# RWKV head pairs: the bonus product placed behind the products of A, and GpSimd's zeros of the first head pair placed behind the spread of the norms

## The chip, the cores and the metric

The kernel runs on one core of a Trainium2 chip. The metric is the device time of one execution in microseconds (us), as the median over several runs. A profiled execution, taken separately, gives the trace.

The engines of the core are named as in the profile: PE is TensorE (PEld its weight loads), DVE is VectorE, ACT is ScalarE, POOL is GpSimd and SP is SyncE, which issues most DMAs.

## What is computed

One layer of a hybrid decoder: RWKV-7 time mixing and differential attention side by side, merged by gates, followed by an MLP. The change lies in the RWKV branch, in the norm of `kk` and in the bonus:

```
r, k, v, wd, ad, gd = jnp.split(Pr, RWKV_SPLITS, axis=-1)
...
kk = hs((k * lp['k_k']).astype(f32))
kk = kk / jnp.maximum(jnp.linalg.norm(kk, axis=-1, keepdims=True), 1e-12)
k = k.astype(f32) * (1.0 + (a - 1.0) * lp['k_a'].astype(f32))
S, y = rwkv7_scan(S0, hs(r), hs(decay), hs(k), hs(v), -kk, kk * hs(a))
...
bonus = jnp.sum(hs(r).astype(f32) * hs(k) * lp['r_k'].astype(f32), axis=-1, keepdims=True) * hs(v).astype(f32)
o = (y + bonus).reshape(B, T, W_A).astype(Pr.dtype) * g
```

`rwkv7_scan` is a recurrence over time with a 64 x 64 state per head. The bonus is needed only at the very end, where it is added to the normalised `y`.

## The kernel before

There are 512 prompt tokens and 64 sample tokens, 576 in a row (`NT`), with features on the partitions. The RWKV branch has eight heads of 64 features, handled as four head pairs `hp` of 128 partitions. The recurrence is done in nine chunks of 64 tokens. For each head pair the generator `rwkv(hp)`, in this order:

- squares `k` (`sq`), sums it over each head on TensorE (`pn`), brings the sums to the power -1/2 on GpSimd (`nr`, L760), spreads them over 64 features on GpSimd (`nb`, L763) and transposes them back on TensorE (`pk`, `pks`); VectorE multiplies them into `kk`, which shares the buffer of `sq`;
- makes the decay (`pw`, `u`, `cum`, `pe`, `pinv`) and the gate `a` (`pa`, `aa`), and the gated key `k2`;
- makes the bonus: `rkp` = r times r_k times k2 on VectorE, its sum over each head by a matmul with a block of ones (`pbn`, two halves), and `bv` = `pbn` times v on VectorE;
- makes the stacked factors `KB` and `ST` (two tiles `ST`, one for each parity of the head in the pair), whose unused rows GpSimd sets to zero (L818);
- makes the products A (`pA`, six banks of PSUM) on TensorE, and from each bank two masked pieces on VectorE: `ABR` and the other rows of `ST`;
- transposes v (`pV`, copied by ACT into `SVU`) and `KB` (`pK`, copied into `KBt`), multiplies the sample states (`pI`), and inverts small triangular blocks in a series of steps (`pW`, `pZ`, `pWc`, `pC`), into `TT`. Parts of `SVU` and `TT` are zeroed, or filled with an identity, by GpSimd (L871, L872, L923, L924).

When two head pairs are ready, `chain(pr)` walks the nine chunks (`pch`, `pY`). After that `pF` updates the sample states: `vm` on GpSimd, `pF` on TensorE, then the update on VectorE, a DMA out (`Ss`) and the DMA in of the next head pair's states.

Between these pieces TensorE works off a stream of dense projections of the gates (`ps_z`, `ps_g`, with weights split into `hi` and `lo`, and results evicted by VectorE into `Z` and `gg`). `take(n)` and `fill(n)` put n steps of the stream at a place of the program; `fill` also keeps them behind the last matmul. The order of instructions on each engine is set by a list scheduler, from the order of the code, from dependencies, and from `tc.issue_after(x)`, which keeps what is issued in its block behind `x` in the order. It adds no wait on the chip. So a piece of code that is moved can shift the order of all engines around it.

`bank` hands out PSUM banks from a ring of three; the stream's banks are a ring of two. `tmp` hands out buffers from a ring of six; `nb` and `vm` share a ring of three (tag G).

Of the kernel before, what the change touches and what calls it, by code (L numbers as in the profile page):

```python
# [8 lines left out]
F32 = mybir.dt.float32  # L9
# [6 lines left out]
P = 128  # L16
# [5 lines left out]
NT = NPR + NS  # L22
# [6 lines left out]
HALF = ((0, 288), (288, 288))  # L29
# [3 lines left out]
V_MU, V_W0, V_A0, V_KK, V_KA, V_RK, V_LW, V_LB, V_GM, V_GF, V_GO, V_SUB, V_END = (  # L33
    0, 14, 18, 22, 26, 30, 34, 38, 42, 50, 58, 66, 67)


C_ID, C_OB, C_M, C_MS, C_LM, C_I32, C_HS, C_SEL, C_MB, C_CM, C_END = (
    0, 128, 256, 384, 512, 672, 704, 706, 738, 746, 748)
# [3 lines left out]
def tile_hybrid_step(ctx, tc, xT, xsT, ktab, vtab, s0T, ptab, w_in, vecs, w2a2, g2, lamv,  # L42
# [3 lines left out]
    PE, VE, AE, GE = nc.tensor, nc.vector, nc.scalar, nc.gpsimd  # L46
    PS = bass.MemoryType.PSUM

    def pool(name, bufs=1, stack=ctx, **kw):
        return stack.enter_context(tc.tile_pool(name=name, bufs=bufs, **kw))  # L50
# [4 lines left out]
    ring = {"job": 0}  # L55

    def act(out, in_, func=AF.Copy, **kw):
        ring["act"] = AE.activation(out=out, in_=in_, func=func, **kw)  # L58

    def tt(out, a, b, op, eng=None):  # L60
        ins = (eng or VE).tensor_tensor(out=out, in0=a, in1=b, op=op)  # L61
        if eng is None:
            ring["tt"] = ins

    def stt(out, a, s, b, op0, op1):
        VE.scalar_tensor_tensor(out=out, in0=a, scalar=s, in1=b, op0=op0, op1=op1)
# [4 lines left out]
    def mm(out, lhsT, rhs, start=True, stop=True):  # L71
        ring["mm"] = PE.matmul(out=out, lhsT=lhsT, rhs=rhs, start=start, stop=stop)  # L72
        return ring["mm"]
# [17 lines left out]
    MUL, ADD, SUB, MAX = ALU.mult, ALU.add, ALU.subtract, ALU.max  # L91
# [9 lines left out]
    def bank(name):  # L101
        return psw.tile([P, 512], F32, tag="w", name=name)
# [9 lines left out]
    c = const.tile([P, C_END], F32, name="cst_sb")  # L112
    nc.scalar.dma_start(out=c, in_=cst)
    ident = c[:, C_ID:C_ID + P]
    onesblk = c[:, C_OB:C_OB + P]
# [18 lines left out]
    def v(i, n=1):  # L134
        return vec[:, i:i + n]
# [135 lines left out]
    with tc.tile_pool(name="xin", bufs=2, reuse_waits="tile") as xin:  # L271
# [6 lines left out]
        for k in range(0, KT, 4):  # L278
            for j in range(3):
                with prio(FEED + 1000 + 10 * k + j):  # L280
                    name = f"raw_{'qkv'[j]}0_{k}"
                    if k == 0:
                        raw = ring["pool"].tile([P, 4, P], F32, tag="raw", name=name, bufs=3)
                    else:
                        raw = zw.tile([P, 1 + NX], F32, tag="z" if j else "tz", name=name,
                                      bufs=2 if j else 1)[:, :4 * P].rearrange("p (k w) -> p k w", k=4)
# [378 lines left out]
    for h in range(HB):  # L665
        if h:
            qkv(h)
        for cc in range(2):
            GE.tensor_copy(
                out=qbd[64 * cc:64 * cc + 64, :, h, 8 * cc:8 * cc + 8],  # L670
                in_=qT[64 * cc:64 * cc + 64, h, NPR:].rearrange("p (b q) -> p b q", b=NB))
# [44 lines left out]
    rb_ = pool("rb_", 2, stack=rk, reuse_waits="tile")  # L716
    rt = pool("rt", 2, stack=rk, reuse_waits="tile")

    def ch(a):
        return a.rearrange("p (c t) -> p c t", t=64)  # L720

    def m3(ap_, n):
        q, w = ap_.shape
        return ap_.rearrange("p (o w) -> p o w", o=1).broadcast_to([q, n, w])
# [17 lines left out]
    def rwkv(hp):  # L742
# [3 lines left out]
        r, k, vv = Pt[hp], Pt[4 + hp], Pt[8 + hp]  # L746

        def tmp(tag, bufs=1):
            return rt.tile([P, NT], F32, tag="T", name=f"{tag}_{hp}", bufs=6)


        sq = tmp("sq")
        act(sq, k, AF.Square, scale=v(V_KK + hp))
        pn = bank(f"pn{hp}")
        for t, o in enumerate(toks):
            mm(pn[:, 2 * t:2 * t + 2], sq[:, o:o + P], c[:, C_HS:C_HS + 2])
        (fill if hp != 2 else take)(8)
        nr = stat.tile([P, 10], F32, tag="nr", name=f"nr{hp}")
# [1 line left out]
        GE.tensor_tensor(out=nr, in0=nr, in1=mhalf[:, :10], op=ALU.pow)  # L760

        nb = rt.tile([P, 5, P], F32, tag="G", name=f"nb{hp}", bufs=3)
        GE.tensor_copy(out=nb.rearrange("p t (a d) -> p (t a) d", a=2),  # L763
                       in_=nr.rearrange("p (a o) -> p a o", o=1).broadcast_to([P, 10, 64]))
        u = tmp("u")
        aa = tmp("aa")
        for t0, n in HALF:
# [31 lines left out]
        k2 = tmp("k2")  # L799
        act(k2, aa, AF.Identity, scale=ka2[:, hp:hp + 1], bias=ka2[:, 4 + hp:5 + hp])  # L800
        tt(k2, k2, k, MUL)
        rkp = tmp("rkp")
        stt(rkp, r, v(V_RK + hp), k2, MUL, MUL)
        bv = rb_.tile([P, NT], F32, tag="bv", name=f"bv{hp}", bufs=4)
        for t0, n in HALF:
            pbn = bank(f"pbn{hp}{t0}")
            mm(pbn[:, :n], onesblk, rkp[:, t0:t0 + n])
            tt(bv[:, t0:t0 + n], pbn[:, :n], vv[:, t0:t0 + n], MUL)


        KB = rt.tile([P, NCH, 2, 64], F32, tag="KB", name=f"KB{hp}", bufs=1)
        stt(aa, aa, 1.0, kk, ADD, MUL)
# [1 line left out]
        for par, rows in halves:  # L814
            stt(KB[rows, :, par], ch(aa)[rows], 0.5, ch(pinv)[rows], MUL, MUL)
            tt(KB[rows, :, 1 - par], ch(k2)[rows], ch(pinv)[rows], MUL)
            st = rb_.tile([P, NCH, 2, 64], F32, tag=f"ST{par}", name=f"ST{par}_{hp}")
            GE.memset(st[64 - 64 * par:128 - 64 * par], 0.0)  # L818
            stt(st[rows, :, 0], ch(kk)[rows], -1.0, ch(pm)[rows], MUL, MUL)
            tt(st[rows, :, 1], ch(r)[rows], ch(pe)[rows], MUL)  # L820
            ST.append(st)
# [4 lines left out]
        for par in range(2):  # L826
            rows = slice(64 * par, 64 * par + 64)
            oth = slice(64 - 64 * par, 128 - 64 * par)
            for c0, cn, mk in ((0, 4, C_M), (4, 4, C_M), (8, 1, C_MS)):
                pA = bank(f"pA{hp}{par}{c0}")  # L830
                for i in range(cn):
                    mm(pA[:, i * P:(i + 1) * P], KBc[c0 + i], ST[par][:, c0 + i])
                pAv = pA[:, :cn * P].rearrange("p (c w) -> p c w", c=cn)
                f2 = lambda a: a[:, c0:c0 + cn].rearrange("p c a t -> p c (a t)")
                tt(f2(ABR)[rows], pAv[rows], m3(c[rows, mk:mk + P], cn), MUL)
                tt(f2(ST[par])[oth], pAv[oth], m3(c[oth, mk:mk + P], cn), MUL)

        yield

# [2 lines left out]
        SVU = own["SVU"][:, :, e]  # L842
# [23 lines left out]
        for par in range(2):  # L866
            rows = slice(64 * par, 64 * par + 64)
            for a in range(2):
                act(ST[par][rows, 8, a].rearrange("p (b t) -> p b t", b=NB),
                    pI[rows, 0:P].rearrange("p (b a t) -> p b a t", b=NB, a=2)[:, :, a])  # L870
            GE.tensor_copy(out=SVU[rows, 8, par], in_=c[rows, C_ID + 64 * par:C_ID + 64 * par + 64])  # L871
            GE.memset(SVU[rows, 0, par], 0.0)  # L872

        yield

# [21 lines left out]
        for l in range(1, 5):  # L897

            n = NCH if l < 3 else 8
# [6 lines left out]
        TT = rb_.tile([P, NCH, 64], F32, tag="TT", name=f"TT{hp}")  # L906
# [12 lines left out]
        for b0, b1 in quads:  # L919
            act(TT[b0, :8, 32:64], pC[b0, :256].rearrange("p (c s) -> p c s", c=8))  # L920
            act(TT[b0, :, 0:32], Y[b0])
            act(TT[b1, :, 32:64], Y[b1])
            GE.memset(TT[b0, 8:, 32:64], 0.0)  # L923
            GE.memset(TT[b1, :, 0:32], 0.0)  # L924

        own[e] = ST, KBt, TT, ABR, pc
        yield
# [113 lines left out]


    gens = [rwkv(hp) for hp in range(4)]

    def run(*stages):
# [78 lines left out]
    for i, d in enumerate((0, 4, 1, 5, 2, 6, 3, 7)):  # L1124
# [31 lines left out]
        for j, (t0, n) in enumerate(HALF):  # L1156
            o = acc[:, t0:t0 + n]
# [142 lines left out]
    rows = []  # L1300
    for d, n in enumerate((None, "t1", "b11", "t2", "b21", "t3", "b22", "t4")):
        if n:
            t = fp.tile([P, 2, 4, 288], F32R, tag=f"h_{n}", name=f"w3_{d}", bufs=1)
            t = t.rearrange("p i k t -> p (i k t)")
# [179 lines left out]
```

## Time and profile before

| | us |
|---|---|
| median of 3 runs | 1003.75 |
| lowest, highest | 1003.34, 1004.62 |
| profiled execution | 1006.88 |
| its span | 1005.1 |
| PE busy, POOL busy | 975.1, 87.5 |

The time on the chip is the time of the slowest engine's chain, here nearly TensorE alone. A row of a timeline gives the start and length in us, the engine, the line of the kernel, the operation, output and inputs, and in brackets how long the engine was idle before it and what released it. A matmul's shown end is modelled, so neighbours on TensorE overlap by the length of the pipeline: the distance between starts is what one costs. A row of the waits gives the total, the number and the longest wait. A row of the windows gives for a stretch the length, then for each engine the busy time and the number of instructions, then the granted clock of TensorE (1.00 is full), the share of the DMA engines and the GB/s.

### The profile page before, as it was taken

What the parts mean: (1) busy time and instruction counts of PE and PEld (TensorE: products, weight loads), DVE (VectorE), ACT (ScalarE), POOL (GpSimd) and SP (SyncE); (2) the same over time, 40 slices, a digit from 0 to 9 for tenths busy, and PEclk for the clock granted to TensorE, in tenths of its full rate; (3) what the DMA queues carried; (4) which work ended last, traced back from release to release, by engine and by line L of the source; (5) the groups of instructions that cost most, each with busy time, mean ns of one, the idle gap of its engine ahead of it and who ended that gap; (6) DMA issues with size and microseconds to landing.
All of it is one profiled execution on the core that took longest, in us unless ns stands there. A gap on an engine that the chain in (4) does not pass through costs nothing.

```text
span 1005.1 us, 24415 instructions
## 1 busy us (share of the span) xinstructions
PE 975.1 (97%) x10012; PEld 919.4 (91%) x10012; DVE 688.9 (69%) x1459; ACT 497.0 (49%) x1094; POOL 87.5 (9%) x171
## 2 busy tenths in 40 slices
PE   9999999899999998999989999999999999999996
PEld 9999998898887887988779999999999999999996
DVE  6698566864946679444579898966666666666644
ACT  6576455354435355453334666644444444444732
POOL 2511001301010340000210000000000000000001
PEclk9999999999989999999999999999999999999999
DMA  7422673211111234323357642222222222221402
GB/s 266 136 70 83 205 223 114 61 64 45 43 59 45 69 106 152 104 81 113 103 182 225 206 140 86 83 95 85 88 92 85 85 84 85 84 87 41 135 3 95
DMA packets 50833, 105.75 MB, mean 105 GB/s; under 512 B 6066, under 2 KB 8114, under 8 KB 50594
## 3 DMA queue, kind: packets, MB, share of 16 engines
q1 hardware_dynamic: 47442, 96.95, 30.4%
q0 software_dynamic: 1648, 5.35, 1.5%
q8 instruction: 79, 1.29, 0.5%
q10 hardware_dynamic: 1632, 1.89, 0.5%
q14 instruction: 32, 0.26, 0.1%
HBM read 89.38 MB, written 14.78 MB: 104 GB/s over the span
## 4 chain that ended last, share of the span: by engine, by line
PE 83%; DVE 6%; ACT 4%; issue 3%; DMA 2%; POOL 1%; SPq 0%; DVEq 0%; ACTq 0%; POOLq 0%
PE ps_dn L72 20%; PE ps_g L72 8%; PE ps_z L72 8%; PE ua L1220 5%; PE ux L1220 5%; PE ps_wo L72 4%; PE ps_k L72 3%; PE uc L1220 3%; PE ub L1220 3%; PE ud L1220 2%; PE ps_bra L72 2%; PE ps_q L72 2%; PE pch L72 2%; PE ps_brb L72 2%; PE ps_v L72 2%
## 5 line engine op out<-in xcount | busy, mean ns | idle before, releaser
L72 PE MATMUL ps_dn<-q,hi_dn 128*128 128x288 f32 x768 | 154.7, 296 | 0.0
L72 PEld LDWEIGHTS ps_dn<-q,hi_dn 128*128 128x128 f32 x768 | 122.7, 188 | 1.4
L72 PE MATMUL ps_dn<-q,lo_dn 128*128 128x288 f32 x384 | 113.2, 295 | 0.0
L72 PE MATMUL ps_g<-xl,hi_g 128*128 128x288 f32 x256 | 79.7, 311 | 0.0
L72 PE MATMUL ps_g<-xh,hi_g 128*128 128x288 f32 x256 | 79.0, 309 | 0.0
L72 PE MATMUL ps_g<-xh,lo_g 128*128 128x288 f32 x256 | 79.0, 309 | 0.0
L72 PEld LDWEIGHTS ps_dn<-q,lo_dn 128*128 128x128 f32 x384 | 72.0, 188 | 0.0
L72 PE MATMUL ps_z<-xh,lo_z 128*128 128x288 f32 (+1 forms) x224 | 68.9, 308 | 0.0
L72 PE MATMUL ps_z<-xh,hi_z 128*128 128x288 f32 (+1 forms) x224 | 67.6, 302 | 0.0
L72 PE MATMUL ps_z<-xl,hi_z 128*128 128x288 f32 (+1 forms) x224 | 66.8, 298 | 0.0
L61 DVE TENSOR_TENSOR ya<-ya,ps_dn 128x288 f32<-128x288 f32 x96 | 43.2, 451 | 29.4 <-PE ps_dn L72 29.4
L58 ACT ACTIVATE hi_dn<-raw_dn 128x512 fp32r<-128x512 f32 x48 | 30.1, 628 | 57.0 <-PE ps_dn L72 57.0
L1220 PE MATMUL ua<-h_b,hi 128*128 128x288 f32 x256 | 53.2, 298 | 0.0
L1220 PE MATMUL ux<-h_t,hi 128*128 128x288 f32 x256 | 52.3, 296 | 0.0
L58 ACT ACTIVATE c<-c 128x288 f32<-128x288 f32 x112 | 48.4, 439 | 7.4 <-DVE c L61 5.8
L72 PEld LDWEIGHTS ps_g<-xh,hi_g 128*128 128x128 f32 x256 | 48.7, 190 | 3.1 <-issue 1.8
L72 PEld LDWEIGHTS ps_g<-xl,hi_g 128*128 128x128 f32 x256 | 48.6, 190 | 1.9
L72 PEld LDWEIGHTS ps_g<-xh,lo_g 128*128 128x128 f32 x256 | 48.6, 190 | 1.6 <-DVE lo_g L61 0.2
L58 ACT ACTIVATE hi<-a 128x1024 fp32r<-128x1024 f32 (+1 forms) x32 | 27.1, 846 | 42.0 <-PE ps_dn L72 34.2
L72 PE MATMUL ps_dn<-q,w 128*128 128x320 f32 (+1 forms) x336 | 46.3, 297 | 0.0
L61 DVE TENSOR_TENSOR lo<-s,hi 128x1024 fp32r<-128x1024 f32 x32 | 39.2, 1224 | 10.1 <-ACT hi L58 10.0
L72 PEld LDWEIGHTS ps_dn<-q,w 128*128 128x128 f32 x336 | 45.3, 190 | 0.1
(395 smaller groups left out, 2802.2 us busy)
## 6 DMA issues: line engine op xcount, KB each, us to landing
a<-in_w_up_dram SPq DMA_DIRECT2D x32, 512.0 KB, 3.4
raw_dn<-in_w_down_dram SPq DMA_DIRECT2D x64, 256.0 KB, 2.8
raw_g<-in_w_in_dram SPq DMA_DIRECT2D x32, 256.0 KB, 3.1
raw_z<-in_w_in_dram SPq DMA_DIRECT2D x28, 256.0 KB, 3.1
gt_d<-gg SPq DMA_DIRECT2D x16, 288.0 KB, 2.4
g<-gt_d SPq DMA_DIRECT2D x16, 288.0 KB, 3.6
kp<-in_ktab_dram SPq DMA_DIRECT2D x16, 256.0 KB, 4.5
vp<-in_vtab_dram SPq DMA_DIRECT2D x16, 256.0 KB, 3.8
```

What stands on the lines that cost most here:

```text
L58: ring["act"] = AE.activation(out=out, in_=in_, func=func, **kw)
L61: ins = (eng or VE).tensor_tensor(out=out, in0=a, in1=b, op=op)
L72: ring["mm"] = PE.matmul(out=out, lhsT=lhsT, rhs=rhs, start=start, stop=stop)
L1220: ring["mm"] = PE.matmul(out=ps[:, :288], lhsT=l[:, k], rhs=hb[blk][:, h, k], start=start and i == 0, stop=i == 11, skip_group_check=skip)
```

## The change

The code of the bonus moves from ahead of `KB` to behind the masks of A, and `pbn` is kept behind the last matmul issued there, the last of A. A function `clear` sets zeros on GpSimd; in head pair 0 it keeps them behind the spread `nb`. The copies of the identity into `SVU` are kept behind the latest `nb` in every head pair.

```diff
+        def clear(a):
+            if hp:
+                GE.memset(a, 0.0)
+            else:
+                with tc.issue_after(ring["nb"].ins):
+                    GE.memset(a, 0.0)
...
-        GE.tensor_copy(out=nb.rearrange("p t (a d) -> p (t a) d", a=2),
-                       in_=nr.rearrange("p (a o) -> p a o", o=1).broadcast_to([P, 10, 64]))
+        ring["nb"] = GE.tensor_copy(out=nb.rearrange("p t (a d) -> p (t a) d", a=2),
+                                    in_=nr.rearrange("p (a o) -> p a o", o=1).broadcast_to([P, 10, 64]))
...
-        rkp = tmp("rkp")
-        stt(rkp, r, v(V_RK + hp), k2, MUL, MUL)
-        bv = rb_.tile([P, NT], F32, tag="bv", name=f"bv{hp}", bufs=4)
-        for t0, n in HALF:
-            pbn = bank(f"pbn{hp}{t0}")
-            mm(pbn[:, :n], onesblk, rkp[:, t0:t0 + n])
-            tt(bv[:, t0:t0 + n], pbn[:, :n], vv[:, t0:t0 + n], MUL)
...
-            GE.memset(st[64 - 64 * par:128 - 64 * par], 0.0)
+            clear(st[64 - 64 * par:128 - 64 * par])
...
                 tt(f2(ST[par])[oth], pAv[oth], m3(c[oth, mk:mk + P], cn), MUL)
+        rkp = tmp("rkp")
+        stt(rkp, r, v(V_RK + hp), k2, MUL, MUL)
+        bv = rb_.tile([P, NT], F32, tag="bv", name=f"bv{hp}", bufs=4)
+        for t0, n in HALF:
+            pbn = bank(f"pbn{hp}{t0}")
+            with tc.issue_after(ring["mm"].ins):
+                mm(pbn[:, :n], onesblk, rkp[:, t0:t0 + n])
+            tt(bv[:, t0:t0 + n], pbn[:, :n], vv[:, t0:t0 + n], MUL)
...
-            GE.tensor_copy(out=SVU[rows, 8, par], in_=c[rows, C_ID + 64 * par:C_ID + 64 * par + 64])
-            GE.memset(SVU[rows, 0, par], 0.0)
+            with tc.issue_after(ring["nb"].ins):
+                GE.tensor_copy(out=SVU[rows, 8, par], in_=c[rows, C_ID + 64 * par:C_ID + 64 * par + 64])
+            clear(SVU[rows, 0, par])
...
-            GE.memset(TT[b0, 8:, 32:64], 0.0)
-            GE.memset(TT[b1, :, 0:32], 0.0)
+            clear(TT[b0, 8:, 32:64])
+            clear(TT[b1, :, 0:32])
```

The order on GpSimd at head pair 0, first before, then now. `ST_0` are the two tiles of head pair 0, `ob_d` is the DMA of the attention's result that is issued from GpSimd's queue; a number behind a name is the tile's.

```order
L711 DMA ob_d<-obs 128x4x64
L818 MEMSET ST_0_2814 64x1152
L818 MEMSET ST_0_2820 64x1152
L760 TENSOR_TENSOR nr_2749<-nr_2749,mhalf 128x10
L871 COPY SVU_2861<-cst_sb 64x64
L872 MEMSET SVU_2861 64x64
L763 COPY nb_2752<-nr_2749 128x640
```

```order
L711 DMA ob_d<-obs 128x4x64
L754 MEMSET SVU_2861 64x64 x2
L768 TENSOR_TENSOR nr_2749<-nr_2749,mhalf 128x10
L771 COPY nb_2752<-nr_2749 128x640
L757 MEMSET ST_0_2805 64x1152
L757 MEMSET ST_0_2811 64x1152
```

The two large zeros now stand behind `nr` and `nb`; two small ones of head pair 1 have come ahead.

The order on VectorE at head pair 1, from the last `KB` on, before:

```order
L61 TENSOR_TENSOR KB_3825<-k_1_3813,pinv_3800 64x9x64
L66 SCALAR_TENSOR_TENSOR rkp_3816<-P_2942,vec,k_1_3813 128x576
L66 SCALAR_TENSOR_TENSOR ST_1_3835<-sq_3726,u_3770 64x9x64
L61 TENSOR_TENSOR ST_1_3835<-P_2942,pe_3795 64x9x64
L61 TENSOR_TENSOR lo_g_1_4061<-raw_g_4_4054,hi_g_1_4060 128x512
L66 SCALAR_TENSOR_TENSOR P_3744<-Z_3474,mu_204,tz_3742 128x512
L66 SCALAR_TENSOR_TENSOR P_3744<-Z_3474,mu_204,tz_3742 128x8x7
L66 SCALAR_TENSOR_TENSOR P_3744<-Z_3474,mu_204,tz_3742 128x8
L61 TENSOR_TENSOR bv_3818<-pbn_3819,P_3086 128x288
```

The end of the same stretch now. Ahead of these rows, behind the last `KB`, stand two `ST`, eight pieces of the masks and one `lo_g`.

```order
L61 TENSOR_TENSOR ABR_3830<-pA_3856,cst_sb 64x512
L61 TENSOR_TENSOR lo_g_0_4255<-raw_g_0_4250,hi_g_0_4254 128x512
L61 TENSOR_TENSOR ST_1_3826<-pA_3856,cst_sb 64x512
L61 TENSOR_TENSOR ABR_3830<-pA_3863,cst_sb 64x128
L61 TENSOR_TENSOR ST_1_3826<-pA_3863,cst_sb 64x128
L66 SCALAR_TENSOR_TENSOR rkp_3867<-P_2942,vec,k_1_3813 128x576
L61 TENSOR_TENSOR Y_4100<-DT_4095,cst_sb 128x288
L66 SCALAR_TENSOR_TENSOR P_3744<-Z_3474,mu_204,tz_3742 128x512
L66 SCALAR_TENSOR_TENSOR P_3744<-Z_3474,mu_204,tz_3742 128x8x7
L66 SCALAR_TENSOR_TENSOR P_3744<-Z_3474,mu_204,tz_3742 128x8
L61 TENSOR_TENSOR bv_3869<-pbn_3870,P_3086 128x288
L61 TENSOR_TENSOR Z_3979<-ps_z_0_3993,R_108 128x288
```

`rkp` stood right behind `KB` and now stands behind sixteen other instructions; the evictions of the stream into `Z` stand behind it.

The order on TensorE around `pbn` of head pair 1, before and now. `pV` are the transposes of v.

```order
L72 MATMUL ps_z_1_3994<-xl,hi_z_1_3989 128x296
L72 MATMUL pbn_3819<-rkp_3816,cst_sb 128x288
L72 MATMUL pbn_3822<-rkp_3816,cst_sb 128x288
L72 MATMUL pA_3840<-ST_1_3829,KB_3825 128x128 x4
L72 MATMUL ps_z_1_3994<-xh,lo_z_1_3990 128x296
```

```order
L72 MATMUL pA_3856<-ST_1_3826,KB_3816 128x128 x4
L72 MATMUL pA_3863<-ST_1_3826,KB_3816 128x128
L72 MATMUL ps_z_1_3994<-xh,lo_z_1_3990 128x296
L72 MATMUL ps_z_1_3994<-xh,hi_z_1_3989 128x296
L72 MATMUL ps_z_1_3994<-xl,hi_z_1_3989 128x296
L72 MATMUL ps_z_1_3994<-xh,lo_z_1_3990 128x296
L72 MATMUL pbn_3870<-rkp_3867,cst_sb 128x288
L72 MATMUL pbn_3873<-rkp_3867,cst_sb 128x288
L76 MATMUL pV_0_3876<-cst_sb,P_3086 128x128 x4
L76 MATMUL pV_448_3885<-cst_sb,P_3086 128x128
```

`pbn` stood ahead of A behind 75 steps of the stream; now 69 steps, the first nine matmuls of A, and then sixteen steps with the rest of A between them stand ahead of it.

The order changes in the other head pairs too. In head pair 2 the four matmuls of `pF` stood in two pairs with six steps of the stream between and 36 behind; now they stand together with 29 behind. Over the whole program the stream is cut into 219 pieces instead of 210. The number of instructions is the same.

## The prediction

> **What bounds the kernel now.** I read the page first: its engines and its chain.
>
> ```profile
> PE 975.1 (97%) x10012; PEld 919.4 (91%) x10012; DVE 688.9 (69%) x1459; ACT 497.0 (49%) x1094; POOL 87.5 (9%) x171
> PE 83%; DVE 6%; ACT 4%; issue 3%; DMA 2%; POOL 1%; SPq 0%; DVEq 0%; ACTq 0%; POOLq 0%
> ```
>
> TensorE is busy for 975.1 of 1005.1 us, so 30 us of its idle time is all that any reordering can recover. The change touches only `rwkv(hp)`, so I asked next what TensorE waits for there, and made a table by stage: head pair 0, head pair 1, the chain between them and head pair 2, and head pair 3.
>
> ```profile
> PE pk L76 <- POOL nb L763: 2.7, 1, 2.7
> PE pbn L72 <- DVE rkp L66: 2.6, 3, 1.8
> ...
> PE pI L72 <- ACT KBt L58: 1.2, 2, 0.8
> ```
>
> ```profile
> core 0: us, PE busy (x) PEld busy (x) DVE busy (x) ACT busy (x) POOL busy (x), PEclk, DMA share, GB/s
> 173.00:207.50 34.50, 30.82 (x244) 28.16 (x242) 27.77 (x58) 14.50 (x29) 11.04 (x22) 1.00 0.22 67
> 250.90:279.60 28.70, 26.80 (x220) 24.43 (x219) 25.91 (x54) 12.61 (x28) 0.91 (x2) 0.95 0.12 38
> 279.60:343.90 64.30, 63.09 (x1167) 53.00 (x1167) 35.68 (x94) 28.39 (x70) 4.81 (x6) 0.97 0.17 55
> 372.00:399.60 27.60, 24.99 (x315) 22.36 (x312) 26.85 (x49) 13.02 (x28) 2.72 (x6) 1.00 0.49 156
> ```
>
> In the second and the last stage VectorE is busy for 25.91 of 28.70 and 26.85 of 27.60 us: there TensorE waits because VectorE is full, and moving a VectorE product only decides which matmul waits. In the chain (third row) TensorE is busy 63.09 of 64.30: there each added piece of TensorE time shows. The granted clock is below 1 in two of these rows; in stretches of 4 us:
>
> ```profile
> 272.00:276.00 4.00, 2.77 (x46) 2.17 (x43) 3.12 (x10) 3.86 (x11) 0.00 (x0) 1.00 0.00 0
> 276.00:280.00 4.00, 4.00 (x59) 3.21 (x61) 2.16 (x7) 1.64 (x7) 1.21 (x1) 0.59 0.00 0
> 280.00:284.00 4.00, 4.00 (x141) 3.66 (x131) 1.49 (x2) 1.25 (x3) 1.46 (x2) 0.55 0.02 4
> ```
>
> Behind a stretch with holes (2.77 of 4 us busy) TensorE ran 8 us at 0.59 and 0.55 of its clock: 0.41 x 4 + 0.45 x 4 = 3.4 us of clock lost, some of it in head pair 1, some in the chain.
>
> **GpSimd's zeros behind nb (head pair 0).** The rows of GpSimd and the transposes that wait for it:
>
> ```profile
> 176.16 0.80 POOL L711 DMA_DIRECT2D ob_d<-obs  x1 [1.33 <-DVE nr L69]
> 177.01 2.16 POOL L818 MEMSET ST<- 64x1152 f32 x2
> 179.14 2.18 POOL L760 TENSOR_TENSOR nr<-nr,mhalf 128x10 f32<-128x10 f32 x1
> ...
> 181.47 0.14 POOL L872 MEMSET SVU<- 64x64 f32 x1
> 181.56 0.71 POOL L763 COPY nb<-nr 128x640 f32<-128x640 f32 x1
> ```
>
> ```profile
> 182.32 0.66 PE L76 MATMUL pk<-cst_sb,nb 128*128 128x128 f32 x4 [2.66 <-POOL nb L763]
> ```
>
> TensorE was free at 182.32 - 2.66 = 179.66. Now the DMA issue stays first (to 177.0), two SVU zeros follow (0.3), nr (2.18), nb (0.71): nb ends at 180.2 instead of 182.3 and the wait is 0.6. That is -2.1 us. The ST zeros (2.16) then run from 180.2 to 182.4, beside VectorE's work on `kk`; The zeros of ST are first read by pA, which stands behind KB and so behind that work; they cost nothing under this cover and would hold pA up without it. VectorE, which idled for pk, then binds (the stage has 27.77 of 34.50 us on it), and some gain can be given back by pA waiting for KB: ends -2.4 and -1.5.
>
> **The bonus product behind A.** No instruction is added. What waited:
>
> ```profile
> 260.59 1.24 PE L72 MATMUL pbn<-rkp,cst_sb 128*128 128x288 f32 x4 [0.61 <-DVE rkp L66]
> 384.37 1.24 PE L72 MATMUL pbn<-rkp,cst_sb 128*128 128x288 f32 x4 [1.82 <-DVE rkp L66]
> ```
>
> In head pair 1 the order puts 16 VectorE instructions between KB and rkp: two products into ST, twelve masks of pA, two lo_g. Their rows, and the chain's rows for TensorE's rates:
>
> ```profile
> 258.93 0.75 DVE L61 TENSOR_TENSOR KB<-k,pinv 64x576 f32<-64x576 f32 x1
> 259.72 0.82 DVE L66 SCALAR_TENSOR_TENSOR rkp<-P,vec,k 128x576 f32<-128x576 f32 x1
> ...
> 262.03 0.69 DVE L61 TENSOR_TENSOR lo_g<-raw_g,hi_g 128x512 fp32r<-128x512 f32 x1
> 262.63 1.08 DVE L66 SCALAR_TENSOR_TENSOR P<-Z,mu,tz 128x512 f32<-128x512 f32 x3
> ...
> 266.45 0.69 DVE L61 TENSOR_TENSOR ST<-pA,cst_sb 64x512 f32<-64x512 f32 x1
> ...
> 268.60 0.28 DVE L61 TENSOR_TENSOR ABR<-pA,cst_sb 64x128 f32<-64x128 f32 x1
> ```
>
> ```profile
> 265.92 1.74 PE ps_g L72 x13
> 267.65 0.89 PE pA L72 x8
> ```
>
> KB ends at 259.7. Twelve large instructions of 0.69 and four of 0.28 make 9.4 us, so rkp starts at 269.1 and ends at 269.9. TensorE starts pA at 259.7 (it waits 0.5 for KB, since 6 stream matmuls fewer stand ahead: 259.98 - 6 x 0.134 = 259.2). Up to pbn it has 36 pA matmuls at 0.89/8 = 0.11 (4.0), 16 of the stream at 1.74/13 = 0.134 (2.1) and three returns between them (0.2 each, below): it is there at 266.4. So pbn waits 3.5 us instead of 0.61. Queued behind pbn on TensorE are pV, the stream, pK and pI. Behind rkp on VectorE now come Y, P, bv and the evictions of ps_z into Z (0.45 + 1.08 + 0.45 + 0.8), to 272.7 instead of 264.8; ACT's activation of Z stands ahead of its SVU copies, and pK behind those: I estimate 0.9 (0.5 to 1.3). Idle 0.5 + 3.5 + 0.9 = 4.9 against 28.70 - 26.80 = 1.9 before is +3.0. Against it: TensorE ran at 0.59 at the end of this stage, and the part of the stage on VectorE ends no later, since its work is the same. The first pW, 279.60 before, can start there again, with pn and pw left over:
>
> ```profile
> 276.45 2.05 PE L72 MATMUL pn<-cst_sb,sq 128*128 128x2 f32 x10
> 278.36 1.31 PE L72 MATMUL pw<-P,wl 128*128 128x288 f32 x2
> ```
>
> Together they took 279.60 - 276.45 = 3.15 us at half clock, so 1.6 at the full one; with pch and pY, also still open (about 1.1), less five more stream matmuls done (0.7), 2.0 us are left over. If the slow clock between 279.6 and 284 (0.45 x 4 = 1.8) goes, only 0.2 is lost. I can't tell which, and take the middle, +1.1 (0.2 to 2.0).
>
> In head pair 3 the wait of 1.82 goes, and pA, first now, waits in its place for KB, which VectorE, busy for 26.85 of 27.60 us, can't bring sooner. The stage can give about VectorE's idle 0.75 and no more: -0.5, ends -1.8 (the whole wait goes) and +0.6 (KB comes that much later than rkp did).
>
> In head pair 2 pbn did not wait. The new order puts pF's four matmuls together and 29 stream matmuls behind, where 6 stood between and 36 behind:
>
> ```profile
> 352.60 1.05 POOL L61 TENSOR_TENSOR vm<-SVU,cst_sb 128x512 f32<-128x512 f32 x1 [1.70 <-PE pF L72]
> ```
>
> ```profile
> 351.38 1.08 PE L72 MATMUL pF<-vm,KBt 128*64 128x512 f32 x4
> 353.39 1.39 PE L72 MATMUL pF<-vm,KBt 128*64 128x512 f32 x4
> 364.44 1.11 PE L72 MATMUL pI<-ST,s 64*64 64x16 f32 x32 [0.66 <-DMA s<-in_s0T_dram]
> ```
>
> The fourth vm starts only when the first pF ends and takes 1.05, which 6 x 0.134 = 0.8 no longer covers: +0.4 (the second pF already took 1.39 for 1.08). From the last pF (354.8) to pI lies a chain of state update, DMA out, DMA in: 9.7 us with 0.66 waiting at its end. With 7 stream matmuls fewer on it (0.9) the wait is 1.6: +0.9 or +1.0. Taken +1.4; ends +0.4 (the DMA comes earlier) and +1.8.
>
> **Cuts of the stream.** TensorE goes 9 more times from the stream to another form and back (by the order, 219 pieces instead of 210), 7 of them in the chain. What a return costs:
>
> ```profile
> 300.03 0.40 PE L72 MATMUL ps_g<-xl,hi_g 128*128 128x288 f32 x1
> 300.27 0.29 PE L72 MATMUL ps_g<-xh,lo_g 128*128 128x288 f32 x1
> 300.40 0.29 PE L72 MATMUL ps_g<-xh,hi_g 128*128 128x288 f32 x1
> ...
> 300.93 0.30 PE L72 MATMUL ps_g<-xl,hi_g 128*128 128x288 f32 x1
> 301.16 0.69 PE L72 MATMUL pC<-Y,Wc 32*32 32x32 f32 x32
> ```
>
> The first matmul after another form is followed after 0.24 instead of 0.13, and the form after the last follows after 0.23: 0.2 a cut, up to 1.8 for nine; as some fall where TensorE waits anyway, +1.1 (0 to 1.8).
>
> **Sum:** -2.1 + 1.1 - 0.5 + 1.4 + 1.1 = +1.0 us. The profiled execution took 1006.88, 3.1 more than the median of 1003.75; the same sum gives 1007.9 under the profiler and 1004.8 as the median.
>
> **Rivals.** *The waits go and nothing takes their place.* The pk wait falls by 2.1 and pbn's 2.6 vanish: 1003.75 - 4.7 = 999.0. For it: both are plain waits of the bound engine, and rkp no longer stands ahead of ST and the masks. Against it: VectorE, full in two of the three places, has the same work.
>
> *The hole slows the clock.* A wait of 3.5 us at pbn is more idle time than the 1.2 us of 272 to 276, behind which the clock fell. A half clock from 269.9 for the same 3.4 us would cost up to 1.7 us, and if the old slow stretch stays as well, head pair 1 costs 2.0 + 1.7 instead of 1.1: +3.6, 1007.4. It decides from a pbn wait of about 3 us in head pair 1; the 2.66 at pk was followed by a clock of 1.00. [...]
>
> *The slow stretch goes.* If TensorE's idle time is now earlier and 273 to 277 is filled with the 20 stream matmuls that the order puts there, the clock stays at 1.00 through the chain, and with half of the hole hidden the sum is 1.0 - 2.4 = -1.4: 1002.4.
>
> **Chances.** Forecast 0.50, own range 1002.7 to 1006.9; waits simply gone 0.20; clock slowed once more 0.15; slow stretch gone 0.15. About 0.2% (2.0 us) is what a measurement can tell from no change. The forecast's half lies 0.02 faster, 0.33 same, 0.15 slower; the first rival is all faster, the second all slower, the third 0.07 faster and 0.08 same: faster 0.29, same 0.41, slower 0.30. Leaving out the outer half of the first rival and of the second gives 1000.2 to 1008.0.
>
> **What the changed profile would show.** pk waits about 0.6 for nb, with GpSimd's ST zeros behind it; the wait of pbn for rkp near 270 is above 3 us; pI waits for the DMA of s by about 1.6; the stage of head pair 3 keeps VectorE full; the clock's low rows lie behind 270 or stay at 276 to 284. I am wrong if pbn never waits, if the scheduler's order leaves VectorE room I counted as full, or if a new wait in the chain adds more than the cuts.

## The result: 0.75% slower, and the profile after

The changed kernel takes 1013.36 us (median of 6 runs, 1008.97 to 1016.13), and the kernel before took 1003.81 in the same measurement. The ratio is 1.0075, with a 95% interval of 1.0057 to 1.0094. Forecast were 1004.8 and a range of 1000.2 to 1008.0. The profiled execution took 1008.97, the fastest of the six, so its trace shows less of the loss than the median does. The granted clock of the six executions lay between 0.986 (the one of 1016.13) and 0.996 (the one of 1009.62): some of the scatter is in the clock.

From the page of the changed kernel, the engines; from its waits, what TensorE waited for longest:

```profile
PE 976.1 (97%) x10012; PEld 918.0 (91%) x10012; DVE 690.1 (69%) x1459; ACT 496.6 (49%) x1094; POOL 91.1 (9%) x171
```

```profile
PE pbn L72 <- DVE rkp L66: 3.6, 1, 3.6
PE pA L72 <- DVE KB L61: 2.3, 3, 1.4
...
PE pk L76 <- POOL nb L771: 1.4, 1, 1.4
...
PE pA L72 <- DVE ST L61: 0.6, 1, 0.6
```

The waits for nb and rkp were 2.7 and 2.6 us, and are 1.4 and 3.6 now; pA's waits for KB and ST are new. Head pair 1 on TensorE and VectorE, and the clock there (windows, columns as before):

```profile
267.66 0.80 DVE L66 SCALAR_TENSOR_TENSOR rkp<-P,vec,k 128x576 f32<-128x576 f32 x1
...
270.32 0.82 DVE L61 TENSOR_TENSOR Z<-ps_z,R 128x288 f32<-128x288 f32 x2
```

```profile
268.61 2.26 PE L72 MATMUL pbn<-rkp,cst_sb 128*128 128x288 f32 x4 [3.56 <-DVE rkp L66]
```

```profile
264.00:268.00 4.00, 1.05 (x9) 0.81 (x7) 3.85 (x8) 1.41 (x4) 0.00 (x0) 0.96 0.16 52
268.00:272.00 4.00, 3.39 (x11) 2.73 (x12) 3.88 (x10) 2.15 (x4) 0.10 (x1) 0.50 0.11 33
272.00:276.00 4.00, 4.00 (x45) 3.84 (x46) 1.95 (x7) 3.21 (x10) 0.00 (x0) 0.68 0.02 4
```

TensorE did 1.05 us of work in the 4 us from 264, while VectorE was full with masks. Behind the hole the clock fell to 0.50, and the four matmuls of pbn took 2.26 us instead of 1.24. In head pair 2 two products on VectorE are longer than in the trace of before:

```profile
345.37 1.49 DVE L66 SCALAR_TENSOR_TENSOR ST<-sq,u 64x576 f32<-64x576 f32 x1
346.78 1.60 DVE L61 TENSOR_TENSOR ST<-P,pe 64x576 f32<-64x576 f32 x1
```

```profile
345.14 4.14 POOL L61 TENSOR_TENSOR vm<-SVU,cst_sb 128x512 f32<-128x512 f32 x3
```

Two products of the same kinds take 0.75 each in the same trace, two to three microseconds earlier. Beside GpSimd's three vm they took twice that, and the three vm took 4.14. Before, vm lay beside the second of these products too, but there the product kept its 0.75 and the three vm took 3.55:

```profile
345.29 0.75 DVE L61 TENSOR_TENSOR ST<-P,pe 64x576 f32<-64x576 f32 x1
```

```profile
345.41 3.55 POOL L61 TENSOR_TENSOR vm<-SVU,cst_sb 128x512 f32<-128x512 f32 x3
```

Three vm take 3.04 in `l1` below, where VectorE's instruction is the longer one: by that, some 0.5 of the 3.55 is waiting, an estimate.

To place the loss I counted every matmul at its usual distance to the next of its kind (0.133 us for the stream, 0.112 for pA, and so on), which gives at each moment the work that TensorE has done, and compared the times at which two executions reach the same work. Worked out so from the traces of the changed kernel and of the run with the zeros alone (below), which differ by 7.4 us in span:

| part of the work | changed, against the zeros alone |
|---|---|
| head pair 0, to the start of head pair 1's products | +0.7 |
| head pair 1, products to the first pW | +3.5 |
| the chain up to head pair 2 | +0.9 |
| head pair 2 | +3.1 |
| head pair 3 | -2.5 |
| second chain | +2.9 |

The parts add up to 8.6; outside them, where the two kernels run the same code, the changed kernel's execution was 1.2 faster. These are two single executions, so a spell of slow clock that one of them had and the other had not is in the numbers.

### The profile page after: what moved, and what is told of

The parts are those of the page before. It is cut to its first block, busy times and chain, and to the rows that moved or that the text cites. A ratio compares the mean times of both kernels' runs of the same rounds, so it can differ in the third digit from the quotient of the medians.

```text
span 1007.2 us, 24422 instructions
## 1 busy us (share of the span) xinstructions
PE 976.1 (97%) x10012; PEld 918.0 (91%) x10012; DVE 690.1 (69%) x1459; ACT 496.6 (49%) x1094; POOL 91.1 (9%) x171
## 4 chain that ended last, share of the span: by engine, by line
PE 84%; DVE 6%; ACT 4%; issue 3%; POOL 2%; DMA 1%; SPq 0%; DVEq 0%; POOLq 0%; ACTq 0%
PE ps_dn L72 20%; PE ps_g L72 10%; PE ps_z L72 7%; PE ua L1231 5%; PE ux L1231 5%; PE ps_wo L72 4%; PE uc L1231 3%; PE ub L1231 3%; PE ps_k L72 2%; PE ps_bra L72 2%; PE ud L1231 2%; PE pch L72 2%; PE ps_q L72 2%; PE ps_v L72 2%; PE pA L72 2%
```

## The experiments

The ratios are to the kernel before, run alongside; each is followed by its 95% interval. Experiments with one letter `l` and a number have the zeros as changed, and the bonus moved in the head pairs named.

### The two parts alone

`e1_zeros_only` has the code of the bonus back ahead of KB and keeps `clear` and the order of SVU's copies. `e2_bonus_only` is the reverse: `clear = lambda a: GE.memset(a, 0.0)`, and the copies without `issue_after`.

> GpSimd's zeros of head pair 0 behind nb, as in the change; the bonus stays ahead of KB. The orders on TensorE and VectorE are those of the kernel before. Theory A (the loss comes from the wait of pbn for rkp in head pair 1 and from slow clock behind it, which the moved bonus makes): this part alone gains the 2 us of pk's wait, about 1002, and scatters no more than before. Theory B (the reshuffled order of the chains, with more cuts of the stream, makes the loss): the same, about 1002. Theory C (the late zeros hold up ST and pA): 1005 or more.

> The bonus behind A as in the change; GpSimd's zeros and copies as before. The order on TensorE is that of the changed kernel. Theories A and B: slower than the changed kernel by what pk's wait costs, 1013 to 1016, with the same wide scatter. Theory C: about 1004 to 1005.

The zeros alone: 1002.09 us, 0.9973 (0.9962 to 0.9984). The bonus alone: 1010.88, 1.0063 (1.0040 to 1.0086). So the zeros gain by themselves and the bonus makes the loss; theory C falls. Theories A and B expected the bonus alone to be slower than the changed kernel, and it is not: 1.0063 against 1.0075, with intervals that overlap.

### Taking the hole away, or filling it

`e3_rkp_early` moves only VectorE's product back, `e4_warm_hole` fills the hole with work:

```diff
         tt(k2, k2, k, MUL)
+        rkp = tmp("rkp")
+        stt(rkp, r, v(V_RK + hp), k2, MUL, MUL)
...
-        rkp = tmp("rkp")
-        stt(rkp, r, v(V_RK + hp), k2, MUL, MUL)
```

```diff
             with tc.issue_after(ring["mm"].ins):
+                for _ in range(8 if hp == 1 and t0 == 0 else 0):
+                    mm(pbn[:, :n], onesblk, vv[:, t0:t0 + n])
                 mm(pbn[:, :n], onesblk, rkp[:, t0:t0 + n])
```

> The changed kernel with only rkp (VectorE) back ahead of KB; pbn and bv stay behind A. VectorE then has rkp done before pbn is reached. The stream is cut into as many pieces as in the change or more (223 against 219 by the order). Theory A: no wait of pbn in head pair 1, no slow clock there, 1001 to 1004 with the narrow scatter of before. Theory B: 1011 to 1014, since the chains are reshuffled as in the change.

> The changed kernel with eight extra matmuls (ones times v, into pbn's own bank, overwritten by the first real pbn) ahead of pbn of head pair 1: 8 x 0.43 = 3.4 us of TensorE work in the hole of 3.56 us. The wait of VectorE's rkp is as long as before, so the stage ends no earlier by it. Theory A, in the form that the clock is what costs: the granted clock holds at 1.00 behind pbn, 1006 to 1010, with less scatter. If only the time of the hole counts, and not the clock: 1012 to 1014 as the changed kernel. Theory B: as the changed kernel.

Both stayed slow: 1012.02, 1.0061 (1.0044 to 1.0078), and 1012.09, 1.0061 (1.0044 to 1.0079). Theory A had 1001 to 1004 and 1006 to 1010, and missed both. In e4's trace the clock held where the hole had been, and fell later in the chain:

```profile
268.00:272.00 4.00, 3.91 (x25) 3.28 (x23) 4.00 (x12) 3.11 (x7) 0.10 (x1) 1.00 0.04 15
272.00:276.00 4.00, 3.83 (x55) 3.51 (x54) 2.51 (x9) 2.91 (x10) 0.00 (x0) 1.00 0.01 4
298.00:302.00 4.00, 4.00 (x45) 2.62 (x42) 0.12 (x1) 1.25 (x3) 1.99 (x2) 0.63 0.07 23
302.00:306.00 4.00, 4.00 (x23) 2.58 (x23) 1.36 (x6) 1.90 (x6) 0.00 (x0) 0.51 0.00 0
```

Filling the hole moved the slow clock and did not measurably change the time. Counted at equal work, with the extra matmuls left out, e4 loses some 1.7 us less than the changed kernel through head pair 1, though rkp comes as late; in the chain, with its spell at 299 us, it loses some 2.7 us more. So in these two traces the slow clock was about half of the 3.5 of head pair 1; what the time would be without any spell in its place, no run shows. In e3 rkp no longer stands among TensorE's waits, but in head pair 2 pA waits 2.3 us at once for a product into ST, which VectorE had begun a moment before GpSimd's vm:

```profile
343.05 3.81 DVE L61 TENSOR_TENSOR ST<-P,pe 64x576 f32<-64x576 f32 x1
```

```profile
343.19 3.04 POOL L61 TENSOR_TENSOR vm<-SVU,cst_sb 128x512 f32<-128x512 f32 x3
```

The product's 0.75 us became 3.81: its own time and the three vm's. Counted at equal work, e3 has lost nothing against the zeros alone up to the start of head pair 2 (0.0 us), and 5.4 us ten microseconds later, where a spell of slow clock follows pA's wait. So with rkp early the loss of head pair 1 is gone, and another one has come.

### One head pair at a time

```diff
+        LATE = (1,)
...
+        if hp not in LATE:
+            bv = bonus(False)
...
+        if hp in LATE:
+            bv = bonus(True)
```

`bonus(late)` holds rkp, pbn and bv, with `issue_after` where late; the run is named by its head pair.

> The kernel with the zeros behind nb (1002.09 in its run), and the bonus moved behind A in head pair 0 alone. Laid beside each other by the work that TensorE has done, the changed kernel's trace loses against the zeros alone: 0.1 us in head pair 0, 3.5 in head pair 1, 0.9 in the first chain, about 3 in head pair 2, gains 2.3 in head pair 3, and loses 2.6 in the second chain. Theory D (each loss comes from its own head pair's bonus): 1002, no change. Theory E (the loss comes from a shifted order in the chains, wherever the shift begins): 1004 or more.

> The zeros behind nb, and the bonus moved in head pair 1 alone. Theory D: the wait for rkp and the chain behind it, 3.5 + 0.9 more than the zeros alone, 1006 to 1007, and the wider scatter. Theory E: as any other single move, 1004 or more, from the chains and not from the wait.

> The zeros behind nb, and the bonus moved in head pair 2 alone. Theory D: about 3 more than the zeros alone, 1005. Theory E: 1004 or more, with the loss outside head pair 2. If the loss of head pair 2 came from what the earlier moves had shifted into it: 1002.

> The zeros behind nb, and the bonus moved in head pair 3 alone. Theory D: 2.3 us gained in head pair 3; if the loss of the second chain belongs to it, 1002.4, and if not, 999.8, faster than either kernel. Theory E: 1004 or more.

| run | us | ratio (interval) |
|---|---|---|
| l0 | 1005.45 | 1.0007 (0.9992 to 1.0022) |
| l1 | 1011.45 | 1.0079 (1.0054 to 1.0104) |
| l2 | 1006.30 | 1.0025 (1.0010 to 1.0041) |
| l3 | 1002.97 | 0.9991 (0.9977 to 1.0006) |

Theory D had 1002 for l0, which took 1005.45; theory E had 1004 or more for l3, which took 1002.97. Neither holds for all four. Against the zeros alone (0.9973), head pair 1 by itself loses as much as the whole change. Theory D missed its size by half (1006 to 1007 expected): laid beside the zeros alone at equal work, l1 loses 3.1 us in head pair 1 and then 5.1 in head pair 2, in which nothing was moved. The rows of l1 there, VectorE, GpSimd and TensorE:

```profile
341.27 0.75 DVE L66 SCALAR_TENSOR_TENSOR ST<-sq,u 64x576 f32<-64x576 f32 x1 [0.47 <-PE pch L72]
...
342.75 0.74 DVE L61 TENSOR_TENSOR ST<-P,pe 64x576 f32<-64x576 f32 x1
...
344.31 3.56 DVE L61 TENSOR_TENSOR lo_g<-raw_g,hi_g 128x512 fp32r<-128x512 f32 x1
```

```profile
342.12 2.17 POOL L754 MEMSET ST<- 64x1152 f32 x2
344.27 3.04 POOL L61 TENSOR_TENSOR vm<-SVU,cst_sb 128x512 f32<-128x512 f32 x3
```

```profile
350.91 1.13 PE L72 MATMUL pA<-ST,KB 128*128 128x128 f32 x8 [2.12 <-DVE ST L61]
```

A lo_g of 0.69 took 3.56, which is about vm's 3.04 and its own time; the ST that pA needs stood behind it. Behind pA's wait the clock fell as well (0.81 and 0.77 in the 8 us from 350), so the 5.1 us are not the collision alone. In l2 a product ST<-P,pe took 3.79 instead of 0.75 and pA waited 2.3 us at the same place, with the clock at 1.00 from 340 to 356; l2 is 5.2 thousandths slower than the zeros alone. Beside GpSimd's memset, at 342.75, VectorE ran at its usual 0.74. In the run with the zeros alone the same three vm lay beside masks of pA, whose one input is in PSUM:

```profile
342.39 3.55 POOL L61 TENSOR_TENSOR vm<-SVU,cst_sb 128x512 f32<-128x512 f32 x3
```

```profile
343.05 0.68 DVE L61 TENSOR_TENSOR ABR<-pA,cst_sb 64x512 f32<-64x512 f32 x1
```

That mask took 0.68, as one does in l1_copy (below) at 349.74, with no vm beside it. So what a shift of VectorE's order by a few microseconds cost here depended on which instruction met vm. Where two such instructions meet, the starts in the rows do not tell which one stands still: the product into ST starts 0.12 us ahead of vm in the trace of before and keeps its 0.75, 0.13 ahead with the zeros alone and keeps 0.76, and 0.14 ahead in e3 and takes 3.81. Beside the products vm, which have two inputs in SBUF, the lo_g took 3.56 against 0.69; beside the memset, which has no input, the product into ST kept its 0.74. Why the two engines held each other up, no run shows.

### Taking the collision away

Two ways: vm as a copy with one input (`GE.tensor_copy(out=vm, in_=m3(SVU[:, 8, par], NB))`, the mask left out), and vm on ACT, with the right result:

```diff
-            tt(vm, m3(SVU[:, 8, par], NB),
-               c[:, C_MB:C_MB + NB].rearrange("p (b o) -> p b o", o=1).broadcast_to([P, NB, 64]), MUL, GE)
+            for b in range(NB):
+                act(vm[:, b], SVU[:, 8, par], AF.Copy, scale=c[:, C_MB + b:C_MB + b + 1])
```

> The run l2 (1006.30; the bonus moved in head pair 2 alone) with one thing changed: vm on GpSimd is a copy with one input instead of a product of two, so the mask of vm is left out. The orders on TensorE and VectorE are those of l2, row for row. In l2 a product ST<-P,pe on VectorE took 3.79 us instead of 0.75, beside GpSimd's vm. Theory F (VectorE's instruction with two operands in SBUF stands still while GpSimd reads two operands): it takes 0.75 again, pA's wait for ST of 2.3 goes, 1003 to 1004. Rival (the shift of TensorE's order makes the loss): 1006.

> The run l1 (1011.45; the bonus moved in head pair 1 alone) with vm as a copy with one input, the mask left out; orders on TensorE and VectorE as in l1. There a lo_g took 3.56 us instead of 0.69 beside vm. Theory F: lo_g takes 0.7, pA's wait for ST of 2.1 goes, 1008 to 1009; the wait for rkp in head pair 1 (3.2) stays. Rival: 1011 to 1012.

> The run l1 with rkp (VectorE) back ahead of KB in head pair 1; pbn and bv stay behind A. TensorE's order is then that of the zeros alone but for 27 rows. Theory D (the wait of 3.2 us and the slow clock behind it, and what is shifted behind them): the wait goes and nothing is shifted into GpSimd's vm, 1002 to 1004. Rival (pbn behind A costs by its place on TensorE, or the shift in the chain is a matter of chance): 1008 or more.

> The control for the two runs with a copy: the zeros alone (1002.09) with vm as a copy with one input, the mask left out; orders on TensorE and VectorE as there. No instruction of VectorE was stretched beside vm in that run, so theory F: 1001.5 to 1002.5. If the copy gains by being shorter than the product: 1000 to 1001, and the two runs are to be read against this.

l2_copy 1004.43, 0.9999 (0.9986 to 1.0013), from 1.0025; l1_copy 1006.88, 1.0020 (1.0008 to 1.0033), from 1.0079; the control l_copy 1002.04, 0.9963 (0.9950 to 0.9977), against 0.9973, so the copy itself gains nothing measurable. Theory F was wrong in one point: a copy with one input holds VectorE up as well, only for less time. In l1_copy:

```profile
345.99 1.71 POOL L957 COPY vm<-SVU 128x512 f32<-128x512 f32 x3
```

```profile
346.04 2.21 DVE L61 TENSOR_TENSOR lo_g<-raw_g,hi_g 128x512 fp32r<-128x512 f32 x1
```

lo_g now takes 2.21, beside three copies of 1.71 together; in l2_copy the product into ST takes 2.43 and pA still waits 1.0 us. The stretch goes with GpSimd's time: 2.9 and 3.0 us of it beside products of 3.04, 1.5 and 1.7 beside copies of 1.71. From l1 to l1_copy the time fell by 5.9 thousandths, more than the 1.4 us by which the stretch shrank; l1_copy's trace has no slow clock from 346 to 362, and the rest was not separated.

l1_early, which has no wait for rkp in head pair 1 and whose order is nearly that of the zeros alone, took 1002.43, 0.9978 (0.9964 to 0.9992): the whole of l1's loss is gone with one VectorE instruction moved back, pbn and bv still behind A. That takes away the hole, the slow clock behind it and the shift into vm together.

In the changed kernel itself, all head pairs moved:

> The changed kernel with vm made on ACT (eight scaled copies each) instead of GpSimd; the result is the same, and TensorE's order is that of the changed kernel but for 6 rows. In its trace two products ST on VectorE took 1.49 and 1.60 us instead of 0.75 beside vm. Theory F: they take 0.75, and 2 to 4 us go, 1008 to 1010; the wait for rkp in head pair 1 stays. Rival (the loss in head pair 2 is TensorE's order): 1012.

> As the run after_act, and rkp of head pair 1 alone back ahead of KB (pbn and bv behind A). If the wait in head pair 1 and the collision in head pair 2 are the two causes in the changed kernel too: 1003 to 1006, what remains being head pair 0's move (3 in its run alone) and the cuts. If the moves of head pairs 0, 2 and 3 cost on their own: 1008 or more.

> The zeros behind nb, the bonus as before, and vm made on ACT. Nothing of VectorE was stretched there, so theory F: 1001 to 1002.5, as the zeros alone (1002.09). If vm on ACT itself costs, by what ACT does late for pF: 1003 or more, and after_act and after_h1_act are to be read against that.

| run | us | ratio (interval) |
|---|---|---|
| changed kernel | 1013.36 | 1.0075 (1.0057 to 1.0094) |
| after_act: vm on ACT | 1008.46 | 1.0037 (1.0023 to 1.0051) |
| after_h1_act: and rkp of head pair 1 early | 1004.15 | 0.9990 (0.9974 to 1.0006) |
| l_act: zeros alone, vm on ACT | 1002.18 | 0.9971 (0.9959 to 0.9984) |

VectorE's two products in head pair 2 of after_act, and TensorE's wait in head pair 1:

```profile
346.03 0.76 DVE L66 SCALAR_TENSOR_TENSOR ST<-sq,u 64x576 f32<-64x576 f32 x1
346.70 0.75 DVE L61 TENSOR_TENSOR ST<-P,pe 64x576 f32<-64x576 f32 x1
```

```profile
269.71 2.26 PE L72 MATMUL pbn<-rkp,cst_sb 128*128 128x288 f32 x4 [3.56 <-DVE rkp L66]
```

All three times lie in the ranges expected from the two causes. The stretch is gone and with it 3.8 thousandths; the hole is as before. The two stretches were only 1.6 us together, so 3.8 is more than VectorE's lost time: after_act also lacks the spell of slow clock that the changed kernel's trace has in head pair 2 (0.76 and 0.81 in the 8 us from 368), and the two were not separated. With rkp early in head pair 1 another 4.7 thousandths go. Of the 10.2 thousandths between the changed kernel and the zeros alone, the two repairs take away 8.5. Both were made by a change that can shift more than its target, so the split between them is that of these kernels. The version that beats both kernels is the zeros alone, 1002.09; vm on ACT adds nothing to it.

## Why the prediction was wrong, step by step

**The zeros: right in kind, half in size.** Forecast -2.1 for pk's wait, measured 2.66 to 1.44, -1.2. nr and nb moved ahead as said, but nb met a scan of VectorE:

```profile
176.73 1.99 POOL L768 TENSOR_TENSOR nr<-nr,mhalf 128x10 f32<-128x10 f32 x1
178.78 1.57 POOL L771 COPY nb<-nr 128x640 f32<-128x640 f32 x1
```

```profile
178.49 1.36 DVE L785 TENSOR_TENSOR_SCAN cum<-reset,u 128x576 f32<-128x576 f32 x1
```

nb took 1.57 instead of 0.71, ending 0.5 us after the scan that had begun before it. I took its duration from a place where VectorE was idle. It may be the same collision the other way round: that is inferred from these rows and was not tried by itself.

**The hole in head pair 1: right, its price wrong.** pbn waits 3.56 us, forecast 3.5. This is the first step that failed: I priced the stage at +1.1, as the middle between the slow clock staying where it was and its going. In fact half clock came right behind the hole and stayed for some 6.8 us (0.96, 0.50 and 0.68 in three windows of 4 us), the stage lost 3.5 against the zeros alone, and bringing rkp back in this head pair gained 4.7 thousandths. The rival of the slowed clock named this, with 3.4 us at half clock and 3.7 us for the stage, and had a chance of 0.15; its total of 1007.4 was too low as well, since it kept the rest of the sum. Its limit of about 3 us of waiting was an estimate; the runs have the four matmuls of pbn at 2.26 us behind a wait of 3.56 (changed kernel, after_act) and behind one of 3.17 (l1). How much of the 3.5 is the clock is not settled: with the hole filled the clock held there, some 1.7 us came back, and went again in the chain. Against the trace of before, where half clock lasted twice as long in this place as with the zeros alone (by the windows 6.8 us against 3.4), the stage lost only some 2 us.

**Head pair 2: the mechanism wrong.** I forecast +1.4 from vm's ring and from the DMA of the states. pF's vm does wait longer (0.7 us against 0.3), but pI waits for no DMA any more. VectorE is held up beside vm, a place where I had looked only at which engine waits for vm. The second step that failed is the assumption that VectorE's durations move with the instruction: they were taken from rows of before, where VectorE lost nothing beside vm, and a stretch was put at nothing. In its place two products took 1.49 and 1.60 instead of 0.75, the stage lost 3.1 us, about 1 of it at a spell of slow clock, and taking vm off GpSimd gained 3.8 thousandths. Against the zeros alone the terms of the bonus were +1.1 - 0.5 + 1.4 + 1.1 = +3.1; measured were 7.4 us in the two traces and 10.2 thousandths in the medians.

**Head pair 0, head pair 3 and the chains.** For the bonus of head pair 0 the sum has no term; l0, which moves it alone, is 3.4 thousandths slower than the zeros alone. Forecast -0.5 for head pair 3 and +1.1 for the cuts. At equal work head pair 3 gains 2.5 and the second chain loses 2.9 again, and l3 shows the same pair, -1.6 and +1.3, with a time that its interval does not tell from the zeros alone. The first chain lost 0.9. The chains' 3.8 against 1.1 is a third term that was too small, and its cause stays open: I did not separate the cuts from the rest of the second chain.

**The naive rival**, 999.0, had the waits simply go; pbn's wait grew. **What stays open:** why l0 costs some 3 us against the zeros alone. Its trace loses between 1 and 2 us at each of two spells of slow clock (one at 208 to 212 us, where the clock is 0.57); no run tried that alone.

## What to carry to other kernels

Before moving work on VectorE by a few microseconds, list what GpSimd reads beside its new place: here five instructions with two operands in SBUF took longer by about the time that GpSimd's products or copies ran (0.7 us became 2.2 to 3.8), two more became 1.49 and 1.60, two others kept 0.75 and 0.76, and a mask with an input in PSUM kept its 0.68. Where VectorE was full, putting a product behind others moved the wait to what needed that product next (pbn waited 3.56 us instead of 0.61). Moving the matmul but leaving its VectorE input early cost nothing in head pair 1 alone (l1_early, 0.9978); in all four head pairs it cost nearly as much as the change (e3, 1.0061), since the shifted order ran into vm (a product of 0.75 us took 3.81). Repeat the timing when TensorE has holes: one profile of a kernel can be its fastest execution.

## What the runs showed of the hardware

VectorE and GpSimd held each other up in these traces: on VectorE 0.69 us became 3.56 beside three products (3.04), 2.21 beside three copies (1.71), and a product stayed at 0.74 beside memsets; where a product kept its 0.75, the three vm on GpSimd took 3.55; nb on GpSimd became 1.57 from 0.71 beside a scan. The clock of TensorE fell to 0.50 for about 3.4 or 6.8 us at a time, at other places in other traces. In l0 0.57 over one window of 4 us alone is (1 - 0.57) x 4 / 0.5 = 3.4 us at half clock. In e3 0.92, 0.50 and 0.72 in windows of 2 us from 276 make 3.4 too. In the changed kernel windows of 1 us show 0.85 at 267, then 0.50 six times, then 0.73: (0.15 + 6 x 0.50 + 0.27) / 0.5 = 6.8. One spell came behind a stretch in which TensorE did little, 1.05 of 4 us, ahead of pbn. But in the trace of before TensorE was busy for 1.66 of the 4 us from 178, and the clock was 1.00 there and up to 207.5; and in e4 the clock fell at about 299 us, behind four windows, from 290 to 298, in each of which TensorE shows as busy for 2.00 of 2 us at a clock of 1.00. What makes it fall, these runs do not show.
